# Seven products of half blocks for gate and up in a hybrid decoder layer

## The chip, the cores and the metric

One core of one Trainium2 chip runs the whole layer as one program. The metric is the device time of one execution in microseconds (us). Engines are named as in the profile: PE (matrix engine), PEld (its weight loads), DVE (vector), ACT (scalar), POOL, SP (which issues most DMAs).

## The reference, cut to what matters

512 tokens, width 1024, one layer, all arrays float32. The attention part in front is the same in both kernels; the change lies in what follows it (2816 hidden columns, that is 22 blocks of 128).

```python
mix = jnp.concatenate([o_a..., o_b...], axis=-1)
h = h + mix @ w_out[layer]
hn = rms_norm(h, norm2_g[layer])
h = h + (jax.nn.silu(hn @ w_gate[layer]) * (hn @ w_up[layer])) @ w_down[layer]
return rms_norm(h, norm_f_g)
```

## The kernel before

**Products in three matmuls.** Every float32 operand is split into a high part (rounded to the fp32r type, a copy on ACT) and a low part (the rest, a subtraction on DVE). A product is then three matmuls, high by high, high by low and low by high, which one PSUM bank adds up: `mm3` (lines 87 to 91, the weight is the stationary operand) and `mm3x` (93 to 97, the activation is). Each matmul has its own load of 128x128 stationary values. `split` (78 to 85) loads 128x512 raw weights by SP and splits them; the letters in `ENG` say which engine does which half.

**Out projection (587 to 604).** Eight steps f, each 128 rows of h1 (features on partitions, 512 tokens in the free dimension). A step loads a partial sum from DRAM (`hp`), does 4 x 3 matmuls of 512 columns, adds on DVE (596), and makes the scaled high and low parts `Xh`, `Xl` on ACT and DVE (598, 599). `turn` (580) transposes h1 on PE to `h1t` (tokens on partitions).

**Gate and up (643 to 666).** For each of 22 blocks j: gate, then up, each 8 x 3 matmuls of 512 columns (`gate_up`, 48 matmuls for a block), with four raw loads of 128x512. `swiglu` (652) does four steps on DVE, a Silu and a copy on ACT, and leaves high and low parts `GH[j]`, `GL[j]`. `second_norm` (626) squares `h1t` on ACT, takes the reciprocal root and spreads it to `R2`, by which both results are multiplied.

**Down (698 to 713).** Two halves c of the 1024 output columns, one after the other; in each, 22 steps k with 4 token tiles x 3 matmuls of 512 columns into four PSUM banks. The last four k are done token tile by token tile, so that `combine` and `finish` of a tile lie beside the next tile's matmuls.

The order of the instructions on each engine comes from a scheduler that the program is built with; tile pools with a fixed number of buffers (`BUFS`, line 39) say how far loads and splits run ahead.

Of the kernel before, what the change touches and what calls it, by code (L numbers as in the profile page):

```python
# [38 lines left out]
BUFS = {"w_raw": 3, "w_hl": 5, "pf": 2, "P": 2, "T": 2, "mf": 1, "oc": 1, "g": 4, "h1": 5, "pair": 1}  # L39
# [13 lines left out]
def tile_hybrid_layer(ctx: ExitStack, tc: tile.TileContext, xT, w_qk0, w_t, w_av, w_vb, w_o, w_gu, w_d,  # L53
# [33 lines left out]
    def mm3(ps, w, sl, xh, xl, first, last):  # L87

        nc.tensor.matmul(ps, w[:, 0, sl], xh, start=first, stop=False)  # L89
        nc.tensor.matmul(ps, w[:, 0, sl], xl, start=False, stop=False)  # L90
        nc.tensor.matmul(ps, w[:, 1, sl], xh, start=False, stop=last)  # L91
# [210 lines left out]
    mixh = act.tile([P, KT, S], F32R, name="act_hi")  # L302
    mixl = act.tile([P, KT, S], F32R, name="act_lo")
# [73 lines left out]
    def blocks(i, wi, tok):  # L377
# [12 lines left out]
        rhl = (mixh if wi == 0 else mixl)[:, 4:8].rearrange("p (x g) s -> p x g s", x=2)  # L390
# [91 lines left out]
    def out_a(f, tok):  # L482
# [3 lines left out]
        for ft in range(4):  # L486
            mm3(ps, w, slice(ft * P, (ft + 1) * P), mixh[:, ft], mixl[:, ft], ft == 0, ft == 3)
# [99 lines left out]
    for f in range(KT):  # L587
        xr = ff.tile([P, S], F32, name="g", bufs=BUFS["g"])
        nc.sync.dma_start(xr, hp[f * P:(f + 1) * P, :])
        w = split(w_o[f, :, 512:1024], 512, *ENG["ob"][:2])  # L590
        ps = bank(("proj", "S")[f % 2])
        for ft in range(4, KT):
            mm3(ps, w, slice((ft - 4) * P, (ft - 3) * P), mixh[:, ft], mixl[:, ft], ft == 4, ft == KT - 1)
        h1 = ff.tile([P, S], F32, name="h1", bufs=BUFS["h1"])
        h1s.append(h1)
        nc.vector.tensor_tensor(out=h1, in0=ps, in1=xr, op=ALU.add)
        g = g_sb[:, 1, f:f + 1]
        nc.scalar.activation(Xh[:, f], h1, AF.Copy, scale=g)
        nc.vector.scalar_tensor_tensor(out=Xl[:, f], in0=h1, scalar=g, in1=Xh[:, f].bitcast(F32), op0=ALU.mult,
                                       op1=ALU.subtract)  # L600
        if f >= DELAY:
            turn(f - DELAY)
    for f in range(KT - DELAY, KT):
        turn(f)
# [56 lines left out]
    for j in range(NJ):
        pg = gate_up(j, 0)
        if j == 0:
            second_norm()
        pu = gate_up(j, 1)
        swiglu(j, pg, pu)


    gf = ff.tile([P, D], F32, name="Xh", bufs=1)
    nc.sync.dma_start(gf, gf_row.to_broadcast([P, D]))  # L670
# [121 lines left out]
```

## Time and profile before

| | |
|---|---|
| three timed runs | 678.35, 681.23, 682.34 us, median 681.23 us |
| the profiled execution | 679.24 us, of which the span of the page is 677.5 us |
| PE busy | 657.1 us, 97% of the span, 3150 matmuls |
| DVE, ACT, POOL busy | 381.5, 305.5, 143.8 us |
| HBM traffic | 106 GB/s over the span |

Matmuls overlap each other in the records, so a busy PE is read by the distance from one start to the next, not by the duration of one. The same holds on DVE where nothing is waited for.

### The profile page before, as it was taken

What the parts mean: (1) busy time and instruction counts of PE and PEld (TensorE: products, weight loads), DVE (VectorE), ACT (ScalarE), POOL (GpSimd) and SP (SyncE); (2) the same over time, 40 slices, a digit from 0 to 9 for tenths busy, and PEclk for the clock granted to TensorE, in tenths of its full rate; (3) what the DMA queues carried; (4) which work ended last, traced back from release to release, by engine and by line L of the source; (5) the groups of instructions that cost most, each with busy time, mean ns of one, the idle gap of its engine ahead of it and who ended that gap; (6) DMA issues with size and microseconds to landing.
All of it is one profiled execution on the core that took longest, in us unless ns stands there. A gap on an engine that the chain in (4) does not pass through costs nothing.

```text
span 677.5 us, 9409 instructions
## 1 busy us (share of the span) xinstructions
PE 657.1 (97%) x3150; PEld 547.0 (81%) x3150; DVE 381.5 (56%) x828; ACT 305.5 (45%) x668; POOL 143.8 (21%) x184
## 2 busy tenths in 40 slices
PE   9999997999999999899999999999999999999995
PEld 6888897888878887778888888888888888888884
DVE  4468776777877679484645555445445532243225
ACT  5544565436765678466433333333333322232214
POOL 6635842253355455320000000000000000000000
PEclk9999998989999999999999999999999999999998
DMA  6766666445236640062222222222223232213213
GB/s 187 225 172 187 174 171 162 126 138 160 79 110 167 208 121 5 1 228 83 94 94 104 98 94 94 100 103 93 94 94 104 98 124 94 93 66 120 94 48 124
DMA packets 47180, 80.13 MB, mean 118 GB/s; under 512 B 7019, under 2 KB 10347, under 8 KB 47132
## 3 DMA queue, kind: packets, MB, share of 16 engines
q1 hardware_dynamic: 46556, 78.48, 37.2%
q10 hardware_dynamic: 576, 1.05, 0.4%
q8 instruction: 25, 0.41, 0.3%
q14 instruction: 23, 0.19, 0.1%
HBM read 66.36 MB, written 5.55 MB: 106 GB/s over the span
## 4 chain that ended last, share of the span: by engine, by line
PE 92%; DVE 3%; ACT 2%; DMA 1%; issue 1%; SPq 0%; ACTq 0%; DVEq 0%
PE proj L89 9%; PE proj L90 9%; PE proj L91 9%; PE PT L89 5%; PE PT L90 5%; PE PT L91 5%; PE S L89 4%; PE S L90 4%; PE S L91 4%; PE PT L340 3%; PE proj L96 2%; PE proj L95 2%; PE proj L97 2%; PE PT L96 2%; PE PT L95 2%; PE PT L97 2%
## 5 line engine op out<-in xcount | busy, mean ns | idle before, releaser
L71 ACT CAST w_hl<-w_raw 128x512 fp32r<-128x512 f32 (+2 forms) x187 | 112.2, 603 | 261.5 <-PE PT L91 62.9
L84 DVE TENSOR_TENSOR w_hl<-w_raw,w_hl 128x512 fp32r<-128x512 f32 (+1 forms) x169 | 116.9, 693 | 145.1 <-ACT w_hl L71 144.6
L84 POOL TENSOR_TENSOR w_hl<-w_raw,w_hl 128x512 fp32r<-128x512 f32 (+1 forms) x47 | 60.9, 1301 | 63.5 <-ACT w_hl L71 26.1
L337 POOL TENSOR_SCALAR P<-P,den 128x512 f32<-128x512 f32 (+1 forms) x96 | 51.5, 558 | 39.1 <-DVE den L329 27.4
L325 ACT ACTIVATE P<-P,mn 128x512 f32<-128x512 f32 (+1 forms) x96 | 53.5, 559 | 12.7 <-DVE mn L323 12.5
L89 PE MATMUL PT<-Xh,w_hl 128*128 128x512 f32 x144 | 56.0, 389 | 0.0
L90 PE MATMUL PT<-Xl,w_hl 128*128 128x512 f32 x144 | 56.0, 389 | 0.0
L91 PE MATMUL PT<-Xh,w_hl 128*128 128x512 f32 x144 | 56.0, 389 | 0.0
L76 DVE TENSOR_TENSOR PTl<-PT,PTh 128x512 fp32r<-128x512 f32 (+2 forms) x96 | 43.8, 482 | 9.7 <-ACT PTh L350 9.3
L323 DVE CUSTOM_DVE_ANT_0 P<-S,T 128x512 f32<-128x512 f32 (+1 forms) x96 | 44.0, 483 | 8.6 <-PE S L318 7.1
L350 ACT CAST PTh<-PT 128x512 fp32r<-128x512 f32 (+2 forms) x96 | 38.1, 426 | 22.3 <-PE PT L340 18.3
L89 PE MATMUL proj<-xh,w_hl 128*128 128x512 f32 x112 | 45.9, 410 | 0.0
L90 PE MATMUL proj<-xl,w_hl 128*128 128x512 f32 x112 | 45.2, 403 | 0.0
L91 PE MATMUL proj<-xh,w_hl 128*128 128x512 f32 x112 | 45.1, 403 | 0.0
L91 PE MATMUL S<-Xh,w_hl 128*128 128x512 f32 x104 | 40.9, 393 | 0.0
L89 PE MATMUL S<-Xh,w_hl 128*128 128x512 f32 x104 | 40.7, 392 | 0.0
L90 PE MATMUL S<-Xl,w_hl 128*128 128x512 f32 x104 | 40.5, 389 | 0.0
L89 PE MATMUL proj<-Xh,w_hl 128*128 128x512 f32 x104 | 40.5, 389 | 0.0
L90 PE MATMUL proj<-Xl,w_hl 128*128 128x512 f32 x104 | 40.5, 389 | 0.0
L91 PE MATMUL proj<-Xh,w_hl 128*128 128x512 f32 x104 | 40.5, 389 | 0.0
L340 PE MATMUL PT<-ident,P 128*128 128x128 f32 x240 | 36.0, 273 | 0.8 <-POOL P L337 0.8
L340 PEld LDWEIGHTS PT<-ident,P 128*128 128x128 f32 x240 | 28.3, 140 | 5.1 <-POOL P L337 1.3
(275 smaller groups left out, 1423.4 us busy)
## 6 DMA issues: line engine op xcount, KB each, us to landing
w_raw<-in_w_gu_dram SPq DMA_DIRECT2D x88, 256.0 KB, 2.7
w_raw<-in_w_d_dram SPq DMA_DIRECT2D x44, 256.0 KB, 2.8
w_raw<-in_w_t_dram SPq DMA_DIRECT2D x28, 256.0 KB, 2.9
T<-gd SPq DMA_DIRECT2D x64, 64.0 KB, 2.0
w_raw<-in_w_o_dram SPq DMA_DIRECT2D x16, 256.0 KB, 3.0
w_raw<-in_w_vb_dram SPq DMA_DIRECT2D x16, 140.0 KB, 2.2
Qb<-in_xT_dram SPq DMA_DIRECT2D x8, 256.0 KB, 3.0
w_raw<-in_w_av_dram SPq DMA_DIRECT2D x8, 256.0 KB, 2.8
```

What stands on the lines that cost most here:

```text
L71: nc.scalar.copy(out, in_)
L76: engines[e].tensor_tensor(out=out, in0=in0, in1=in1, op=op)
L84: engines[lo].tensor_tensor(out=w[:, 1, :n], in0=raw[:, :n], in1=w[:, 0, :n].bitcast(F32), op=ALU.subtract)
L89: nc.tensor.matmul(ps, w[:, 0, sl], xh, start=first, stop=False)
L90: nc.tensor.matmul(ps, w[:, 0, sl], xl, start=False, stop=False)
L91: nc.tensor.matmul(ps, w[:, 1, sl], xh, start=False, stop=last)
L95: nc.tensor.matmul(ps, xh, w[:, 0, sl], start=first, stop=False)
L323: nc.vector.tensor_tensor_reduce(out=pp, in0=sv, in1=T[:, S - w:], op0=ALU.add, op1=ALU.min, scale=1.0, scalar=3e38, accum_out=mn[:, t:t + 1])
L325: nc.scalar.activation(pp, pp, AF.Exp, bias=mn[:, t:t + 1], scale=-1.0, accum_out=den[:, t:t + 1])
L337: nc.gpsimd.tensor_scalar(pp, pp, den[:, t:t + 1], 1.0, op0=ALU.mult, op1=ALU.mult)
L340: nc.tensor.transpose(pv[:, kb * P:(kb + 1) * P], pp[:, kb * P:(kb + 1) * P], ident)
L350: nc.scalar.copy(ov[0], pv)
```

## The change

The attention part keeps its instructions (two tiles are cut in four, with other names). In the feed-forward part:

- **Seven products.** The gate and up weights of a block and the two halves of the 1024 features are taken as a 2x2 matrix of blocks, the features by the two halves of the tokens as another. Instead of eight block products (128 columns out, 512 features, 256 tokens) there are seven, of sums and differences of blocks. So a block j has 7 x 4 x 3 = 84 matmuls of 256 columns instead of 48 of 512.
- **Sums of weights.** `weights(j)` loads the same four 128x512 pieces, forms four sums of them on DVE, and splits seven pieces instead of four, four of them in pairs of 128x1024.
- **Blocks of x.** `lower` and `upper` make the seven blocks of x from h1 in the out projection, in place of `Xh` and `Xl`: per f<4 two scaled copies and one cast on ACT and four steps on DVE, per f>=4 one scaled copy and one cast of 768 columns on ACT and five steps on DVE, all beside the add of h1.
- **Results.** Partial sums stay in PSUM and are added to by later products; three of them are copied out by ACT, five steps of 256 columns and one of 512 on DVE finish a block. The result stays in fp32; `split_g` splits it in the down stage.
- **Down.** One pass over k with both column halves, so all eight PSUM banks are in use; w_down is loaded as 128x1024. h1t goes to DRAM after the second norm (four DMAs of 512 KB) and comes back in the down stage.

```diff
-BUFS = {"w_raw": 3, "w_hl": 5, "pf": 2, "P": 2, "T": 2, "mf": 1, "oc": 1, "g": 4, "h1": 5, "pair": 1}
+BUFS = {"w_raw": 3, "w_hl": 5, "pf": 2, "P": 2, "T": 2, "mf": 1, "oc": 1, "g": 3, "h1": 4, "pair": 1, "raw2": 6, "hl2": 3, "xe": 4, "xf": 4}
...
+    def lower(k):
+
+        h, g, n = h1s[k], g_sb[:, 1, k:k + 1], ng[:, k:k + 1]
+        e = ff.tile([P, 2, HS], F32, name="xe", bufs=BUFS["xe"])
+        nc.scalar.activation(e[:, 1], h[:, HS:], AF.Copy, scale=g)
+        nc.vector.scalar_tensor_tensor(out=e[:, 0], in0=h[:, :HS], scalar=n, in1=e[:, 1], op0=ALU.mult, op1=ALU.add)
+        nc.scalar.activation(X1[0][:, k, 0], h[:, :HS], AF.Copy, scale=n)
+        nc.vector.scalar_tensor_tensor(out=X1[1][:, k, 0], in0=h[:, :HS], scalar=n, in1=X1[0][:, k, 0].bitcast(F32),
+                                       op0=ALU.mult, op1=ALU.subtract)
+        copy("a", X1[0][:, k, 1], e[:, 0])
+        tt("v", X1[1][:, k, 1], e[:, 0], X1[0][:, k, 1].bitcast(F32), ALU.subtract)
+        return e
+
+    def upper(k, e):
...
+        nc.vector.scalar_tensor_tensor(out=f[:, 0], in0=h[:, HS:], scalar=g, in1=e[:, 0], op0=ALU.mult, op1=ALU.subtract)
+        nc.vector.scalar_tensor_tensor(out=f[:, 1], in0=h[:, HS:], scalar=n, in1=e[:, 1], op0=ALU.mult, op1=ALU.add)
+        nc.vector.scalar_tensor_tensor(out=f[:, 2], in0=h[:, :HS], scalar=g, in1=f[:, 0], op0=ALU.mult, op1=ALU.subtract)
+        b = X2[0][:, k, 0:2].rearrange("p a n -> p (a n)")
+        nc.scalar.activation(b, h, AF.Copy, scale=n)
+        nc.vector.scalar_tensor_tensor(out=X2[1][:, k, 0:2].rearrange("p a n -> p (a n)"), in0=h, scalar=n,
+                                       in1=b.bitcast(F32), op0=ALU.mult, op1=ALU.subtract)
+        copy("a", X2[0][:, k, 2:5], f)
+        tt("v", X2[1][:, k, 2:5], f, X2[0][:, k, 2:5].bitcast(F32), ALU.subtract)
...
+    def weights(j):
+
+        l0 = raw2()
+        nc.sync.dma_start(l0[:, 0], w_gu[j, 0, :, 0:WC])
...
+        tt("v", l0[:, 1], c, d, ALU.add)
+        w0 = split2(l0, "a", "v")
+        yield {"a": w0[:, :, 0], "S1": w0[:, :, 1]}
+        l1, l2 = raw2(), raw2()
+        nc.sync.dma_start(l1[:, 1], w_gu[j, 0, :, WC:])
+        tt("v", l1[:, 0], l0[:, 1], l0[:, 0], ALU.add)
+        w1 = split2(l1, "a", "v")
+        tt("v", l2[:, 0], l1[:, 0], l1[:, 1], ALU.add)
+        tt("v", l2[:, 1], c, l0[:, 0], ALU.add)
+        yield {"S2": w1[:, :, 0], "b": w1[:, :, 1], "S4": split1(l2[:, 0], "a", "v"), "S3": split1(l2[:, 1], "a", "v"),
+               "d": split1(d, "a", "v")}
+
+    def product(ps, w, X, b, first):
+
+        for k in range(HK):
+            mm3(ps, w, slice(k * P, (k + 1) * P), X[0][:, k, b], X[1][:, k, b], first and k == 0, k == HK - 1, True)
...
+        product(u["A"], u["w"]["a"], X1, 0, True)
+        nc.scalar.copy(u["q1"], u["A"])
+        product(u["C"], u["w"]["S1"], X1, 1, True)
+        nc.scalar.copy(u["p5"], u["C"])
+        return u
+
+    def second_part(j, u):
...
+        product(u["A"], u["w"]["S2"], X2, 2, False)
+        nc.scalar.copy(u["u2"], u["A"])
+        product(u["B"], u["w"]["b"], X2, 0, True)
+        tt("v", y[:, :HS], u["B"], u["q1"], ALU.add)
+        product(u["C"], u["w"]["S4"], X2, 1, False)
+        tt("v", y[:, HS:], u["C"], u["u2"], ALU.add)
+        product(u["A"], u["w"]["S3"], X2, 3, False)
+        tt("v", z[:, HS:], u["A"], u["p5"], ALU.add)
+        tt("v", y, y, R2, ALU.mult)
+        nc.scalar.activation(y, y, AF.Silu, scale=-1.0)
+
+    def third_part(j, u):
+        y, z = u["y"], zs[j]
+        product(u["A"], u["w"]["d"], X2, 4, False)
+        tt("v", z[:, :HS], u["A"], y[:, :HS], ALU.mult)
+        tt("v", z[:, HS:], z[:, HS:], y[:, HS:], ALU.mult)
...
+    second_part(0, units[0])
+    third_part(0, units[0])
+    for j in range(1, NJ):
+        if j > 1:
+            units[j] = first_part(j)
+            third_part(j - 1, units[j - 1])
+        second_part(j, units[j])
+    third_part(NJ - 1, units[NJ - 1])
...
+        copy("a", GH[k], zs[k])
+        tt("v", GL[k], zs[k], GH[k].bitcast(F32), ALU.subtract)
...
+        if k < NJ - LAST:
+            for c in range(2):
+                for t in range(NT):
+                    down(ps, t, c, k, w)
```

How the change moves instructions, at the three places that the prediction speaks of.

DVE at the end of the out projection, before: `h_...` is h1 of one f, `Xl` the low parts, `w_hl` low parts of weights, `h1t` the transposed h1.

```order
L596 TENSOR_TENSOR h_3511<-proj,g 128x512
L84 TENSOR_TENSOR w_hl<-w_raw,w_hl 128x512
L599 SCALAR_TENSOR_TENSOR Xl<-h_3511,g_sb,Xh 128x512
L596 TENSOR_TENSOR h_3541<-S,g 128x512
L73 COPY h1t<-PT 128x4x128
L84 TENSOR_TENSOR w_hl<-w_raw,w_hl 128x512
L599 SCALAR_TENSOR_TENSOR Xl<-h_3541,g_sb,Xh 128x512
```

The same place now (`X_3331` holds the low parts of five of the blocks, `xf` the sums they come from, `raw_3681` the weights of block j=1):

```order
L651 TENSOR_TENSOR h_3597<-S,g 128x512
L632 SCALAR_TENSOR_TENSOR xf<-h_3561,g_sb,xe 128x256
L633 SCALAR_TENSOR_TENSOR xf<-h_3561,ng,xe 128x256
L634 SCALAR_TENSOR_TENSOR xf<-h_3525,g_sb,xf 128x256
L637 SCALAR_TENSOR_TENSOR X_3331<-h_3561,ng,X_3330 128x512
L76 TENSOR_TENSOR X_3331<-xf,X_3330 128x768
L632 SCALAR_TENSOR_TENSOR xf<-h_3597,g_sb,xe 128x256
L633 SCALAR_TENSOR_TENSOR xf<-h_3597,ng,xe 128x256
L634 SCALAR_TENSOR_TENSOR xf<-h_3561,g_sb,xf 128x256
L637 SCALAR_TENSOR_TENSOR X_3331<-h_3597,ng,X_3330 128x512
L76 TENSOR_TENSOR X_3331<-xf,X_3330 128x768
L634 SCALAR_TENSOR_TENSOR xf<-h_3597,g_sb,xf 128x256
```

From the last add of h1 to the last low part of x there were three steps; now there are thirteen and a tiny one (two more of 768 columns follow the rows shown), and only then come the sums of the weights of block 1.

ACT at the same place now (`g,ss<-h1t` are the squares of the second norm, `h1t<-PT` the copies of the transposes, `X_3330` high parts of blocks, `xf<-S` a partial sum from PSUM):

```order
L636 ACTIVATE X_3330<-h_3597,ng 128x512
L71 COPY h1t<-PT 128x4x128
L71 CAST X_3330<-xf 128x768
L657 ACTIVATE g,ss<-h1t 128x512 x4
L721 COPY xf<-S 128x256
L723 COPY xf<-proj 128x256
L657 ACTIVATE g,ss<-h1t 128x512 x2
L71 CAST X_3330<-xf 128x768
L657 ACTIVATE g,ss<-h1t 128x512
L71 CAST X_3330<-xf 128x768
```

The casts of the last two steps' high parts (k=2 and 3) stand behind six and seven squares; before, the last high part of x stood ahead of all squares but one.

DVE in the middle of gate and up, before, one block j (`G_3573` is a result's low part):

```order
L84 TENSOR_TENSOR w_hl<-w_raw,w_hl 128x512
L76 TENSOR_TENSOR g<-S,R_3570 128x512
L84 TENSOR_TENSOR w_hl<-w_raw,w_hl 128x512
L76 TENSOR_TENSOR g<-g,R_3570 128x512
L84 TENSOR_TENSOR w_hl<-w_raw,w_hl 128x512
```

And now, most of one block (`raw_...` sums of weights, `hl_...` low parts of a pair, `act_...` the fp32 result):

```order
L76 TENSOR_TENSOR raw_5432<-w_raw,raw_5421 128x512
L76 TENSOR_TENSOR g<-proj,xf 128x256
L76 TENSOR_TENSOR g<-g,R_3337 128x512
L76 TENSOR_TENSOR hl_5301<-raw_5294,hl_5301 128x1024
L76 TENSOR_TENSOR raw_5421<-w_raw 128x512
L76 TENSOR_TENSOR raw_5431<-raw_5421 128x512
L76 TENSOR_TENSOR act_3772<-S,xf 128x256
L76 TENSOR_TENSOR raw_5432<-raw_5431 128x512
L76 TENSOR_TENSOR w_hl<-raw_5305,w_hl 128x512
L76 TENSOR_TENSOR act_3772<-act_3772,g 128x256
L76 TENSOR_TENSOR g<-PT,xf 128x256
L76 TENSOR_TENSOR hl_5308<-raw_5304,hl_5308 128x1024
```

A block had eight DVE steps of 512 columns; it has fifteen now: eight of 512, two of 1024, five of 256, and steps that wait for PE stand between those that make the next block's weights.

## Rows read from the trace of the kernel before

**Rows 1.** The page: busy time of the engines, and the chain that ended last by engine.
```profile
PE 657.1 (97%) x3150; PEld 547.0 (81%) x3150; DVE 381.5 (56%) x828; ACT 305.5 (45%) x668; POOL 143.8 (21%) x184
...
PE 92%; DVE 3%; ACT 2%; DMA 1%; issue 1%; SPq 0%; ACTq 0%; DVEq 0%
```
**Rows 2.** Windows: gate and up, then down; busy us and count by engine, granted clock, DMA.
```profile
304.78:544.60 239.82, 239.82 (x1063) 198.30 (x1062) 123.27 (x194) 90.95 (x156) 0.00 (x0) 1.00 0.28 96
544.60:669.30 124.70, 124.70 (x536) 100.11 (x534) 39.65 (x65) 33.34 (x61) 0.00 (x0) 1.00 0.26 89
```
**Rows 3.** PE in order of time, gate and up: start, us, instruction (22 matmuls, 21 steps).
```profile
360.22 0.39 PE L91 MATMUL PT<-Xh,w_hl 128*128 128x512 f32 x1
...
364.98 0.39 PE L91 MATMUL S<-Xh,w_hl 128*128 128x512 f32 x1
```
**Rows 4.** PE in order of time, narrower matmuls: 280 columns (nine steps), then 256.
```profile
126.02 0.29 PE L97 MATMUL proj<-w_hl,xl 128*128 128x280 f32 x1
...
127.17 0.29 PE L97 MATMUL proj<-w_hl,xl 128*128 128x280 f32 x1
...
128.06 0.28 PE L317 MATMUL S<-KDb,Qb 128*128 128x256 f32 x1
128.18 0.28 PE L318 MATMUL S<-KL,Qb 128*128 128x256 f32 x1
```
**Rows 5.** One line's instructions: weight loads of the 280-column matmuls, ns min/median/max.
```profile
L95 PEld LDWEIGHTS proj<-w_hl,xh x48: 186/188/193, 14.1 to 131.2; 128*128 128x128 f32 x48
```
**Rows 6.** Groups by form on DVE: busy us, mean ns, idle before and its releaser.
```profile
L84 DVE TENSOR_TENSOR w_hl<-w_raw,w_hl 128x512 fp32r<-128x512 f32 x70 | 48.5, 693 | 47.2 <-ACT w_hl L71 46.9
...
L76 DVE TENSOR_TENSOR PTl<-PT,PTh 128x256 fp32r<-128x256 f32 x24 | 10.0, 416 | 0.5 <-ACT PTh L350 0.5
...
L76 DVE TENSOR_TENSOR act_hi<-Qb,act_hi 128x1024 fp32r<-128x1024 f32 x1 | 1.2, 1225 | 0.1
```
**Rows 7.** DVE in order of time: steps that wait for nothing, in three places.
```profile
134.70 0.47 DVE L282 SCALAR_TENSOR_TENSOR vb<-proj,rstd_t,vb 128x256 fp32r<-128x256 f32 x1
135.09 0.41 DVE L323 CUSTOM_DVE_ANT_0 P<-S,T 128x256 f32<-128x256 f32 x1
...
178.99 0.42 DVE L76 TENSOR_TENSOR PTl<-PT,PTh 128x256 fp32r<-128x256 f32 x1
179.33 0.42 DVE L458 TENSOR_TENSOR cy<-S,cy 128x256 f32<-128x256 f32 x1
...
300.49 0.68 DVE L84 TENSOR_TENSOR w_hl<-w_raw,w_hl 128x512 fp32r<-128x512 f32 x1
301.09 0.74 DVE L599 SCALAR_TENSOR_TENSOR Xl<-h,g_sb,Xh 128x512 fp32r<-128x512 f32 x1
301.75 0.68 DVE L596 TENSOR_TENSOR h<-proj,g 128x512 f32<-128x512 f32 x1
```
**Rows 8.** Out projection: DVE's first add of h1, PE's last matmul there, its first of gate.
```profile
290.39 0.69 DVE L596 TENSOR_TENSOR h<-proj,g 128x512 f32<-128x512 f32 x1 [4.84 <-PE proj L91]
...
303.76 0.39 PE L91 MATMUL S<-act_hi,w_hl 128*128 128x512 f32 x1
...
304.78 0.47 PE L89 MATMUL S<-Xh,w_hl 128*128 128x512 f32 x1
```
**Rows 9.** ACT in order of time: two squares of the second norm.
```profile
311.31 0.62 ACT L612 ACTIVATE g<-h1t 128x512 f32<-128x512 f32 x1
...
311.92 0.61 ACT L612 ACTIVATE g<-h1t 128x512 f32<-128x512 f32 x1
```
**Rows 10.** Windows in front of the out projection's last steps.
```profile
284.00:286.20 2.20, 0.21 (x1) 0.00 (x0) 0.68 (x1) 1.20 (x2) 0.00 (x0) 0.99 0.00 0
286.20:289.60 3.40, 3.35 (x8) 2.69 (x9) 0.00 (x0) 0.39 (x1) 1.27 (x1) 0.50 0.29 64
```
**Rows 11.** The end, in order of time: PE's last matmul and the last DMA issue.
```profile
668.98 0.40 PE L97 MATMUL O<-w_hl,G 128*128 128x512 f32 x1
...
673.61 0.37 ACTq L688 DMA_DIRECT2D out_dram<-h1t  x1
```

More of the change, by code (lines that the diff above doesn't have):

```diff
@@ L85, in split, with mm3 @@
         return w
[L87 to L91, printed above, removed]
+    def mm3(ps, w, sl, xh, xl, first, last, skip=False):
+        nc.tensor.matmul(ps, w[:, 0, sl], xh, start=first, stop=False, skip_group_check=skip)
+        nc.tensor.matmul(ps, w[:, 0, sl], xl, start=False, stop=False, skip_group_check=skip)
+        nc.tensor.matmul(ps, w[:, 1, sl], xh, start=False, stop=last, skip_group_check=skip)
     def mm3x(ps, xh, xl, w, sl, first, last):
@@ L594, in tile_hybrid_layer @@
         h1 = ff.tile([P, S], F32, name="h1", bufs=BUFS["h1"])
-        h1s.append(h1)
+        h1s[f] = h1
         nc.vector.tensor_tensor(out=h1, in0=ps, in1=xr, op=ALU.add)
[L597 to L604, printed above, removed]
@@ L661, in tile_hybrid_layer @@
[L661 to L670, printed above, removed]
-    def w_down(k, c):
-        return split(w_d[k * P:(k + 1) * P, c * HD:(c + 1) * HD], HD, *ENG["d"])
-    def down(ps, t, k, w):
-        tk = slice(t * P, (t + 1) * P)
-        mm3x(ps[t], GH[k][:, tk], GL[k][:, tk], w, slice(0, HD), k == 0, k == NJ - 1)
@@ new lines, in second_part @@
+    def second_part(j, u):
+        if j == 16:
+            Z = ff.tile([P, KT, S], F32, name="h1t", bufs=1)
+            zs.extend(Z[:, i] for i in range(NJ - 16))
+        y, z = u["y"], zs[j]
[9 more added lines that the diff above has]
+        nc.scalar.activation(y, y, AF.Silu, scale=-1.0)
@@ new lines, in third_part @@
+    def third_part(j, u):
+        y, z = u["y"], zs[j]
+        product(u["A"], u["w"]["d"], X2, 4, False)
+        tt("v", z[:, :HS], u["A"], y[:, :HS], ALU.mult)
+        tt("v", z[:, HS:], z[:, HS:], y[:, HS:], ALU.mult)
+    es = []
+    for f in range(KT):
+        out_b(f)
+        if f < HK:
+            es.append(lower(f))
+        else:
+            upper(f - HK, es[f - HK])
+            done = nc.cur_bb.bb.instructions[-1]
+        if f >= DELAY:
+            turn(f - DELAY)
+        if f == 2:
+            ahead = weights(0)
+            w0 = next(ahead)
@@ new lines, in tile_hybrid_layer @@
+    for f in range(KT - DELAY, KT):
+        turn(f)
+    w0.update(next(ahead))
+    units = {0: first_part(0, w0)}
+    with tc.issue_after(done):
+        units[1] = first_part(1)
+    second_norm()
+    quads = ["act00", "act01", "act10", "act11"]
+    zs = [q[:, i] for tag in quads for q in [act.tile([P, 4, S], F32, name=tag)] for i in range(4)]
+    second_part(0, units[0])
[5 more added lines that the diff above has]
+        second_part(j, units[j])
@@ new lines, in tile_hybrid_layer @@
+    for t in range(NT):
+        for c in range(2):
+            for i, k in enumerate(range(NJ - LAST, NJ)):
+                down(ps, t, c, k, ws_last[i])
+            x = cell(t, c)
+            nc.vector.scalar_tensor_tensor(out=x, in0=ps[c][t], scalar=nrstd_t[:, t:t + 1], in1=x, op0=ALU.mult,
+                                           op1=ALU.add)
+            square(t, c, x)
+            if c == 0:
+                tt(ENG["c"], x, x, gf[0], ALU.mult)
+        rsqrt(slice(t, t + 1), rstd_t)
```

174 lines of the change are left out of this document (101 added, 73 removed), and 2 rows, old and new, of the table ENG.

## The prediction

> **What bounds the kernel now.** I read the page first: PE is busy for 97% of the span, and the chain that ended last is PE for 92% [rows 1]. So the time is PE's stream of matmuls plus a few gaps, and the other engines matter where they make PE wait. The windows by stage show that nothing does so in the two stages that are changed: gate and up is one unbroken run of 239.82 us, down one of 124.70 us, at the full clock, with DVE busy for 123.27 us and ACT for 90.95 us of the first [rows 2]. A busy PE says nothing about its pace, so I took that from start to start: 21 steps in 4.76 us, 0.2267 us for a matmul of 512 columns [rows 3]. The attention part keeps its instructions and their order, so I leave it alone.
>
> **PE's work in gate and up.** Before: 22 blocks x 48 = 1056 matmuls x 0.2267 = 239.4 us, which is the window [rows 2]. Now: 22 x 84 = 1848 matmuls of 256 columns. The stage has none of that width, but attention does: two stand 0.12 us apart, and nine steps of 280 columns take 1.15 us, 0.1278 each [rows 4]. Taking off 24 columns at the pace that lies between 280 and 512 (0.0989 us for 232 columns, 0.43 ns each) gives 0.1176. I take 0.118: 218.1 us, a gain of 21.3 us. Bounds: 0.117 (216.2 us, gain 23.2) and 0.1278, since narrower can't be slower than 280 columns (236.2 us, gain 3.2).
>
> What speaks against this: the weight loads grow from 1056 to 1848. A load of the 280-column matmuls lasts 0.188 us [rows 5], yet those matmuls follow each other after 0.1278 us, so loads overlap each other as well as matmuls, and a load's duration is not its price. The Trainium skill (Perfetto Trace Analysis, Identifying the Most-Contended Engine) says that the busy share of weight loads, not of matmuls, is the measure of how near PE is to its limit. By that rule 1848 loads of 0.188 us, 347 us, would be the stage, and the change a large loss; the rows above speak against it, and it is a rival below.
>
> **DVE's work in gate and up.** A block has fifteen steps: eight of 512 columns, two of 1024, five of 256. By their durations, 0.693, 1.225 and 0.416 us [rows 6], that is 10.07 us, against 84 x 0.118 = 9.91 us of PE: DVE would be the bound. But the duration is the distance only where a step waits. Where steps wait for nothing, the next starts 0.60 us after one of 512 columns, 0.34 after one of 256 [rows 7], some 0.08 us sooner; for 1024 I take 1.14. That makes 4.80 + 2.28 + 1.70 = 8.8 us, about 9.1 with two steps a block that need the one before them. So DVE is 92% busy where it was half busy. The Trainium skill (VectorE: DVE Perf Modes, The DRAIN you can't avoid) says that a step does not start until the pipe of the one before is empty. By it a block would cost the 10.07 us; the rows show the earlier starts, so I keep 9.1, and 10.07 is the upper bound.
>
> The weight buffers hold about one block ahead, so small waits are absorbed. Price of what is not: between 0 and (10.07 - 9.91) x 21 = 3.4 us, more if waits come on top (a rival). I take 2.
>
> **The start of gate and up.** Here I see the largest loss. Before, DVE followed PE closely through the out projection, and gate began 1 us after the last matmul there [rows 8]. Now DVE has, from its first add of h1 at 290.39 [rows 8], 49 steps before the last block of x is split: 15 plain ones of 512 columns, 20 scaled ones of 256, 4 scaled ones of 512, 4 plain ones of 256, 2 of 1024, 4 of 768. At spacings of 0.60, 0.39, 0.66, 0.34 [rows 7], 1.14 and about 0.87 (between 512 and 1024) this is 9.0 + 7.8 + 2.6 + 1.4 + 2.3 + 3.5 = 26.6 us: 317 us on this trace's clock if it never waits. It does wait: the last two casts on ACT stand behind the squares, at 0.62 us each [rows 9], so I put the last low part at 320.
>
> PE is through with the out projection at 304. Until 320 it can do only what block 0 offers, 72 matmuls (8.5 us) and four groups of transposes (1.6 us; two such groups fill the 0.8 us between the stages [rows 8]), the last 15 of them after 320, so it reaches 322 with some 8 us lost. Behind that DVE makes the weights of blocks 1 and 2 (another 20 steps or so, until about 333), which PE could use sooner: some 3.5 us more. I take 11.5 us lost. Bounds: 4 us, if ACT and DVE overlap better than I counted and PE fills in, and 20 us, if waits on ACT stretch the 49 steps by a third. PE idles in pieces; when it idled for 2.2 us before, the granted clock was 0.50 for the next 3.4 us and eight matmuls took them all [rows 10], which is inside the upper bound.
>
> **The rest.** Down keeps its 528 matmuls: 124.70 us for the window, 0.2327 us each with edges [rows 2]. A step k now has 24 of them, 5.6 us, against 1.225 + 0.693 = 1.9 us on DVE [rows 6] for splits of 1024 and 512 columns, and two copies of the same widths on ACT, so the splits are hidden, and three steps' weights are split before the 18 late results come. If that cover went, it would show as PE gaps at k=3. The pace went from 0.227 in gate to 0.233 in down with the same shapes, so other buffers may move it by 0.006 either way, 3 us; I take 0. Joining the stages costs nothing now; the last product of block 21 waits for DVE once, beside which down's first matmuls are queued: 0.5 us. From PE's last matmul to the last issue were 4.6 us [rows 11], by the same kinds of steps: 0. The four stores of h1t and their reloads stand in SP's queue ahead of loads for block 2 and k=12; both are needed some 8 us later: 0, or 1 us in the ramp, inside its bounds.
>
> **Sum.** -21.3 + 2 + 11.5 + 0.5 = -7.3 us on the profiled execution's own 679.24 us: 672 us. That execution lies 2 us under the median of the runs shown, 681.23, and within their range.
>
> **Rivals.**
> - *PE is hardly held at the start*: 4 us instead of 11.5, no loss in the blocks. For it: DVE idled 4.84 us before its first add of h1 [rows 8], so the stage had room. -21.3 + 4 + 0.5 gives 662 us, with the lower bound of the matmuls 660.
> - *DVE sets the pace, mildly*: a block takes 10.2 us, the durations of rows 6 and a little waiting. 21 x 0.29 = 6 us instead of 2: 676 to 678 us, no change that can be told.
> - *DVE sets the pace with waits* (the other side): PE's results and the next weights stand in one DVE queue. A step that waits for PE holds up the weights behind it, PE then comes late, and the next step waits again. It decides from a block time of 10.25 us (7.3 us over 21 blocks, beside the 2 that I gave); with one such wait of 0.5 us on top of 10.07 it is 10.57, 14 us over 21 blocks instead of 2: 684 us. For it: DVE's mean wait behind an ACT cast is already 0.67 us a step before (47.2 us, 70 steps [rows 6]). Against it: the buffers hold a block.
> - *Weight loads set the pace*, as the rule on their busy share has it: 1848 x 0.188 = 347 us, 107 us more than before, some 786 us. Only the 280-column rows stand against it, and they are enough for me.
>
> **How the numbers follow.** 0.5% is about what a measurement of this kernel can tell from no change, 3.4 us. The forecast (667 to 676) has 0.46, little loss at the start 0.21, mild DVE pace 0.15, DVE pace with waits 0.16, weight loads 0.02. Faster: 0.46 + 0.21 and a little of the mild case, 0.68; same 0.14; slower 0.18. The forecast's own range is 667 to 676; to hold 8 in 10 it reaches down to most of the first rival, 661, and up through the mild case to the third rival's price, 684.
>
> **What would show it.** Right: about 1848 matmuls of 256 columns, 0.118 us apart; DVE over 85% busy in gate and up; PE gaps that end on DVE low parts between 304 and 335 us of the span, few later; a block of 9.9 to 10 us. Wrong: a block of over 10.25 us with PE waiting for DVE throughout, matmuls more than 0.125 us apart without a gap, or a down stage that is not 123 to 126 us.

## The result, and the profile after

The changed kernel takes 671.51 us (median of 4 runs, 670.78 to 672.42) beside 680.45 us (678.35 to 682.34) of the kernel before: a ratio of 0.987, 95% interval 0.9836 to 0.9903. A second set of runs, taken later, gave 0.9869 (0.9846 to 0.9893). It is faster by 1.3%, 9 us; the prediction was 672.0.

The page of the changed kernel (span 669.5 us), busy times and the chain that ended last, to be read against [rows 1]:

```profile
PE 640.4 (96%) x3942; PEld 570.6 (85%) x3942; DVE 478.1 (71%) x994; ACT 353.1 (53%) x745; POOL 143.5 (21%) x184
...
PE 84%; DVE 7%; ACT 3%; issue 2%; DMA 1%; POOL 0%; SPq 0%; DVEq 0%; ACTq 0%; POOLq 0%
```

PE still has most of the chain, but 84% of it where it had 92%; DVE and ACT have taken over that part. Where they did so is seen in windows: the start of gate and up in two pieces, the steady middle, and down (columns as in [rows 2]).

```profile
304.60:322.00 17.40, 12.81 (x76) 11.96 (x74) 15.36 (x28) 14.57 (x33) 0.00 (x0) 0.71 0.31 122
322.00:345.00 23.00, 21.86 (x175) 20.77 (x174) 23.00 (x43) 15.04 (x25) 0.00 (x0) 1.00 0.37 126
```
```profile
400.00:500.00 100.00, 100.00 (x846) 100.00 (x845) 92.68 (x152) 53.99 (x91) 0.00 (x0) 1.00 0.32 109
```
```profile
545.00:661.90 116.90, 114.46 (x498) 93.06 (x497) 46.35 (x64) 37.98 (x58) 0.00 (x0) 1.00 0.25 88
```

In the middle PE does 846 matmuls in 100 us, 0.118 us each, without a gap, and DVE is 93% busy beside it. In the first 17.4 us PE does 76 matmuls where that pace would give 147, at a mean clock of 0.71. The list of what PE waited for (us in total, times, longest) over the whole feed-forward part is short:

```profile
PE PT L612 <- DVE h L651: 3.3, 1, 3.3
PE S L96 <- DVE hl L76: 1.6, 1, 1.6
PE PT L90 <- DVE X L637: 1.3, 1, 1.3
PE S L95 <- ACT hl L71: 0.8, 1, 0.8
PE proj L91 <- DVE hl L76: 0.6, 1, 0.6
PE S L89 <- ACT xf L721: 0.5, 1, 0.5
PE S L89 <- ACT xf L732: 0.5, 1, 0.5
```

The first, the third and the last lie at the start; the second and fourth (L95 and L96 are the down stage) at step k=3 of down; the other two are single waits in later blocks, at 342 and 365 us. The start in more detail, windows first, then DVE's last steps for x in order of time:

```profile
309.00:312.45 3.45, 0.12 (x3) 0.03 (x1) 3.45 (x7) 1.43 (x3) 0.00 (x0) 0.81 0.00 0
312.45:316.90 4.45, 3.22 (x14) 2.92 (x14) 4.45 (x10) 3.94 (x10) 0.00 (x0) 0.50 0.45 178
316.90:321.40 4.50, 4.48 (x19) 4.24 (x20) 2.46 (x5) 4.48 (x13) 0.00 (x0) 0.50 0.74 294
```
```profile
311.62 0.68 DVE L651 TENSOR_TENSOR h<-S,g 128x512 f32<-128x512 f32 x1
...
319.86 0.96 DVE L76 TENSOR_TENSOR X<-xf,X 128x768 fp32r<-128x768 f32 x1 [1.73 <-ACT X L71]
...
321.21 0.96 DVE L76 TENSOR_TENSOR X<-xf,X 128x768 fp32r<-128x768 f32 x1 [0.32 <-ACT X L71]
322.08 0.68 DVE L76 TENSOR_TENSOR raw<-w_raw 128x512 f32<-128x512 f32 x1
```

PE waits from 309 to 312.45: the transposes of the last step's h1 are next in its queue, and the last add of h1 comes only at 311.62, 7.0 us after PE began the last matmul of the out projection (304.58): it stands in DVE's queue behind steps for x and for the weights of block 0. Then the granted clock is 0.50 for some 10 us, and DVE finishes the last x block at 322.2.

A balance, worked out from the starts of the matmuls in the two traces. From the first matmul of gate to the last of down it was 364.20 us and is 356.77, 7.4 us less; the rest of the 8.0 us between the spans lies in front (the first matmul comes 0.4 us later) and behind (from the last matmul to the end 7.6 us, before 8.5). Groups of 84 matmuls, one block's worth, from start to start:

```
21.05 10.76 10.67 9.96 10.70 9.99 9.97 9.97 9.97 9.97 9.96 ... 9.97 9.96 us
```

| | before | after | difference, us |
|---|---|---|---|
| gate and up at their steady pace | 1056 x 0.2267 = 239.4 | 1848 x 0.1186 = 219.2 | -20.2 |
| gate and up beyond that pace (nearly all in the first six groups) | 1.9 | 13.8 | +11.9 |
| down at its pace, from its first start to its last | 122.9 (0.233 a matmul) | 121.0 (0.230) | -1.9 |
| down, waits at k=3 | 0 | 2.8 | +2.8 |
| sum | 364.2 | 356.8 | -7.4 |

### The profile page after: what moved, and what is told of

The parts are those of the page before. It is cut to its first block, busy times and chain, and to the rows that moved or that the text cites. A ratio compares the mean times of both kernels' runs of the same rounds, so it can differ in the third digit from the quotient of the medians.

```text
span 669.5 us, 11165 instructions
## 1 busy us (share of the span) xinstructions
PE 640.4 (96%) x3942; PEld 570.6 (85%) x3942; DVE 478.1 (71%) x994; ACT 353.1 (53%) x745; POOL 143.5 (21%) x184
## 4 chain that ended last, share of the span: by engine, by line
PE 84%; DVE 7%; ACT 3%; issue 2%; DMA 1%; POOL 0%; SPq 0%; DVEq 0%; ACTq 0%; POOLq 0%
PE proj L89 8%; PE proj L91 8%; PE proj L90 8%; PE S L89 6%; PE S L90 6%; PE S L91 6%; PE PT L340 3%; PE proj L96 3%; PE proj L95 3%; PE proj L97 3%; PE PT L96 2%; PE PT L97 2%; PE PT L95 2%; PE PT L89 2%; PE PT L90 2%
## 5 line engine op out<-in xcount | busy, mean ns | idle before, releaser
L76 DVE TENSOR_TENSOR hl<-raw,hl 128x1024 fp32r<-128x1024 f32 x64 | 77.8, 1219 | 53.7 <-ACT hl L71 49.2
L71 ACT CAST hl<-raw 128x1024 fp32r<-128x1024 f32 x64 | 67.1, 1051 | 61.9 <-PE O L97 57.5
L71 ACT CAST w_hl<-w_raw 128x512 fp32r<-128x512 f32 (+2 forms) x76 | 43.3, 576 | 59.9 <-PE S L91 18.9
L325 ACT ACTIVATE P<-P,mn 128x512 f32<-128x512 f32 (+1 forms) x96 | 53.5, 559 | 12.6 <-DVE mn L323 12.3
L76 DVE TENSOR_TENSOR PTl<-PT,PTh 128x512 fp32r<-128x512 f32 (+2 forms) x96 | 43.8, 482 | 9.6 <-ACT PTh L350 9.2
L89 PE MATMUL S<-X,hl 128*128 128x256 f32 x176 | 50.0, 284 | 0.5 <-ACT xf L721 0.5
L89 PE MATMUL S<-X,w_hl 128*128 128x256 f32 x176 | 49.7, 283 | 0.5 <-ACT xf L732 0.5
L90 PE MATMUL S<-X,w_hl 128*128 128x256 f32 x176 | 49.8, 283 | 0.0
L90 PE MATMUL S<-X,hl 128*128 128x256 f32 x176 | 49.7, 282 | 0.0
L91 PE MATMUL S<-X,w_hl 128*128 128x256 f32 x176 | 49.7, 283 | 0.0
L91 PE MATMUL S<-X,hl 128*128 128x256 f32 x176 | 49.5, 281 | 0.0
L71 ACT CAST w_hl<-raw 128x512 fp32r<-128x512 f32 x45 | 27.3, 619 | 35.5 <-PE S L91 28.3
L90 PE MATMUL proj<-xl,w_hl 128*128 128x512 f32 x112 | 45.5, 406 | 0.0
L84 DVE TENSOR_TENSOR w_hl<-w_raw,w_hl 128x512 fp32r<-128x512 f32 (+1 forms) x37 | 26.0, 708 | 14.7 <-ACT w_hl L71 14.4
L89 PEld LDWEIGHTS S<-X,hl 128*128 128x128 f32 x176 | 33.9, 192 | 0.9 <-ACT xf L721 0.9
```

Of the source, the lines that this page charges most:

```text
L71: nc.scalar.copy(out, in_)
L76: engines[e].tensor_tensor(out=out, in0=in0, in1=in1, op=op)
L84: engines[lo].tensor_tensor(out=w[:, 1, :n], in0=raw[:, :n], in1=w[:, 0, :n].bitcast(F32), op=ALU.subtract)
L325: nc.scalar.activation(pp, pp, AF.Exp, bias=mn[:, t:t + 1], scale=-1.0, accum_out=den[:, t:t + 1])
```

## The experiments

Two theories of the loss at the start stood against each other: DVE's steps for x hold PE (the prediction), or something beside them does, namely the fall of the clock, ACT's squares, or late transfers. Two more questions were the price of a narrow matmul and how near DVE is to setting the pace. Where a difference is under 2 us, the distance from the first matmul of gate to the last of down is given beside the ratio (356.8 us for the changed kernel, 357.3 in its second profile), since the first matmul of gate lies anywhere from 302.9 to 307.9 us from one profile to another (308.2 in experiment 9, whose edit reaches in front of it).

**1. The price of halves alone.** The kernel before, its 512-column matmuls cut in two:

```diff
-                mm3(ps, w, slice(k * P, (k + 1) * P), Xh[:, kt], Xl[:, kt], kt == 0, kt == KT - 1)
+                for b in (slice(0, S // 2), slice(S // 2, S)):
+                    mm3(ps[:, b], w, slice(k * P, (k + 1) * P), Xh[:, kt, b], Xl[:, kt, b], kt == 0, kt == KT - 1)
...
```

> The kernel before, with every 512-column matmul of gate and up made as two of 256 columns, so 2112 matmuls and 2112 weight loads in place of 1056; nothing is left out. PE pace theory: a matmul of 256 columns costs 0.118 to 0.119 us, so the stage takes 249 to 251 us in place of 239.4, and the kernel 10 to 11 us longer than the one before: 690 to 692 us beside 680.5. Weight-load theory (a load of 0.188 us is the price): 2112 x 0.188 = 397 us, some 157 us longer, about 838 us.

Measured: 1.0186 of the kernel before (1.0159 to 1.0212), 11 to 14 us longer, a little more than expected. One thing the expectation leaves unsaid: both halves sum in one bank with a start of their own, and gate and up come out with other values; the number, size and loads of the matmuls are as stated. Gate and up in one window:

```profile
304.00:560.00 256.00, 256.00 (x2124) 255.06 (x2123) 126.25 (x197) 92.73 (x160) 0.00 (x0) 1.00 0.29 92
```

The weight loads are busy for 99.6% of it and yet the matmuls follow each other after 0.120 us, though a load lasts 0.19 us. So 1056 more loads with the same columns cost 14 us (378.1 us from first to last matmul, 364.2 before), not 157: the rival in which the duration of the loads sets the pace is out. It also shows the price of the change's shape: a half costs 0.1186 to 0.120 us, not half of 0.2267, so seven eighths of the work bring 8.4% and not 12.5%.

**2. Without the low parts of x.** Of `lower` and `upper` the four steps that make low parts go, and the product reads the high part twice:

```diff
-        nc.vector.scalar_tensor_tensor(out=X1[1][:, k, 0], in0=h[:, :HS], scalar=n, in1=X1[0][:, k, 0].bitcast(F32),
-                                       op0=ALU.mult, op1=ALU.subtract)
...
-        tt("v", X2[1][:, k, 2:5], f, X2[0][:, k, 2:5].bitcast(F32), ALU.subtract)
...
-            mm3(ps, w, slice(k * P, (k + 1) * P), X[0][:, k, b], X[1][:, k, b], first and k == 0, k == HK - 1, True)
+            mm3(ps, w, slice(k * P, (k + 1) * P), X[0][:, k, b], X[0][:, k, b], first and k == 0, k == HK - 1, True)
```

> The changed kernel without the low parts of the seven x blocks: the sixteen DVE steps that make them are left out, and the matmuls that read them read the high parts instead, so PE's work is the same and the result is less exact. DVE theory (its steps ahead of the last x block hold PE): 8 x 0.37 + 4 x 0.66 + 4 x 0.87 = 9.1 us less on DVE before PE can go on, so the loss of some 12 us at the start falls to about 3 to 4: 661 to 664 us. Rivals in which DVE is not what holds PE (late raw weights, ACT's order, the clock): 669 to 672 us.

Measured: 0.9822 (0.9783 to 0.986), 670.45 us; 354.1 us from first to last matmul. About 3 us, not 9: the expectation missed, and the windows show why.

```profile
304.60:322.00 17.40, 16.56 (x135) 15.88 (x134) 14.23 (x25) 17.37 (x38) 0.00 (x0) 1.00 0.61 214
322.00:345.00 23.00, 17.23 (x119) 15.74 (x118) 18.79 (x37) 11.39 (x18) 0.00 (x0) 0.85 0.25 91
```

PE does 135 matmuls until 322 in place of 76, as the theory has it (some of them because gate begins 2.3 us sooner in this profile), but then 119 in place of 175. In order of time on PE:

```profile
327.11 0.39 PE L89 MATMUL S<-X,w_hl 128*128 128x256 f32 x1 [1.39 <-DVE act L76]
...
333.19 2.08 PE L137 MATMUL O<-g,ones 128*128 128x512 f32 x2 [4.38 <-DVE g L134]
```

L137 spreads the second norm's factors. It stands in PE's queue ahead of work that could run, and its input is made by the last (L134) of six DVE steps, five of them tiny, which stand between large ones from 321 to 333. Taking one wait away uncovered the next. Nor did all of the gain fall at the start: PE's waits at k=3 of down are gone in this run too, and down is 1.4 us shorter (2.8 us of waits less, at a slower pace, as in experiment 10), so the start itself gave back only 1.3 of the 2.7 us.

**3. PE kept busy.** 32 matmuls that nobody reads, where PE waits:

```diff
+    full = filler(14, last_pe())
+    with tc.issue_after(full):
+        turn(KT - 1)
+    full = filler(18, last_pe())
...
```

> The changed kernel with 32 added matmuls of 512 columns whose result nobody reads, 14 ahead of the transposes of the last h1 step and 18 behind them (7.3 us of PE), put where PE waits at the start of gate and up; nothing is left out. Clock theory: the 10.2 us at half clock there are the loss, matmuls took 0.213 us in place of 0.118; with the clock kept up the kernel gains 3 to 4.5 us: 667 to 668.5 us. DVE theory: PE can go on only when DVE has split the last x block at about 322 of the span, whatever its clock until then: 671 to 672.5 us, with the granted clock at 1.00 from 309 to 322.

Measured: 0.9871 (0.985 to 0.9893), as the changed kernel; 357.2 us from first to last matmul, also the same.

```profile
308.00:312.45 4.45, 4.45 (x36) 4.22 (x35) 4.45 (x9) 3.47 (x7) 0.00 (x0) 1.00 0.01 4
312.45:316.90 4.45, 4.03 (x21) 3.09 (x20) 4.45 (x10) 2.67 (x4) 0.00 (x0) 1.00 0.00 0
316.90:322.00 5.10, 5.10 (x33) 4.57 (x32) 3.99 (x7) 5.07 (x16) 0.00 (x0) 1.00 0.72 287
```

The clock stays at 1.00, 7.3 us of useless matmuls are taken in, and the time does not change. That the fill itself is not the new limit is seen in one wait that is left: PE still waits 0.6 us for the last low part of x (L90 for DVE's L76). So the half clock of the changed kernel cost nothing that this can tell: PE ran slowly in time that it had to wait in anyway. The changed kernel's second profile agrees: its clock over 304.6 to 322 is 0.80 in place of 0.71, and from first to last matmul it takes 357.3 us in place of 356.8.

**4. Squares behind the casts.**

```diff
...
-    second_norm()
+    with tc.issue_after(cast):
+        second_norm()
```

> The changed kernel with the squares of the second norm queued on ACT behind the last cast of an x block; nothing is left out. ACT theory: the casts behind the squares are the larger part of the loss, 5 us or more back: under 667 us. DVE theory: only the 1.73 and 0.32 us for which DVE waited for these casts come back, 1 to 2 us: 669.5 to 670.5 us; and R2 comes later, so a new wait of PE for results of blocks 0 and 1 may take it back: then 671.5 us or above.

Measured: 0.9874 (0.9856 to 0.9893), no gain; 358.6 us from first to last matmul, 1.8 more. PE's waits:

```profile
PE PT L612 <- DVE h L651: 3.3, 1, 3.3
PE S L89 <- ACT xf L732: 1.8, 1, 1.8
...
PE S L91 <- DVE hl L76: 1.4, 1, 1.4
PE O L137 <- DVE g L134: 1.0, 1, 1.0
...
PE PT L90 <- DVE X L637: 0.3, 1, 0.3
```

The wait for x falls from 1.3 to 0.3 us, and in its place stand a wait for the norm (L137) and two others. ACT's order by itself is not the loss.

**5. Both taken away: low parts and second norm.** Kernel 2 without `square`, `rsqrt` and `spread` in `second_norm`, factors set to ones.

> The changed kernel without the low parts of the x blocks and without the second norm (squares, reciprocal root, the matmul that spreads R2 and its copy are left out, R2 and the token factors are ones); the matmuls of the products stay. Theory: at the start DVE's steps ahead of the last x block and, behind them, the second norm's chain of small DVE steps hold PE one after the other; with both gone PE loses 1 to 4 us of the 12 between the out projection and 345 of the span, 8 to 11 us less than the changed kernel: 0.971 to 0.975 of the kernel before. Rival, raw weights that arrive late behind the stores of h1t, or ACT's casts, hold it as well: PE still waits 5 us or more there, 0.977 or above.

Measured: 0.9706 (0.9683 to 0.973), 661.07 us; 344.2 us from first to last matmul, 12.6 less than the changed kernel. The only waits of PE left in the feed-forward part, and the two windows:

```profile
PE PT L89 <- ACT hl L71: 0.2, 1, 0.2
PE S L89 <- ACT hl L71: 0.2, 1, 0.2
```
```profile
304.60:322.00 17.40, 17.01 (x134) 16.16 (x133) 16.89 (x31) 14.46 (x26) 0.00 (x0) 1.00 0.41 154
322.00:345.00 23.00, 23.00 (x196) 23.00 (x195) 21.76 (x38) 13.92 (x23) 0.00 (x0) 1.00 0.48 152
```

134 and 196 matmuls, though gate begins 2.3 us later in this profile: nothing is left of the loss, so late transfers are no third cause, and ACT's casts of the x blocks, with no squares ahead of them here, hold nothing either. Of the 12.6 us, 1.4 lie in down, where the waits at k=3 are gone as in experiment 2; 11.2 lie at the start.

**6. Only the second norm taken away.**

> The changed kernel without the second norm alone (squares, reciprocal root, the matmul that spreads R2 and its copy are left out, R2 and the token factors are ones); the low parts of the x blocks stay. Together the two were worth 0.0163 of the kernel before, 11 us (0.9869 to 0.9706), the low parts alone 0.0047, 3 us. Theory, two limits one behind the other (first DVE's steps ahead of the last x block, then the norm's chain): without the norm alone the first limit stays, and only the 2.05 us that DVE waits for casts behind squares and 0.9 us of the spreading matmuls can come back, 1 to 4 us: 0.981 to 0.986. Rival, the two add up: the norm alone is worth 0.0163 - 0.0047, 8 us: 0.973 to 0.977.

Measured: 0.9825 (0.9801 to 0.9849); 353.6 us from first to last matmul. Low parts alone are worth 0.0047, the norm alone 0.0044, both together 0.0163 of 681 us, that is 3.2, 3.0 and 11.1 us. They do not add up: one stands behind the other, and removing either leaves most of the loss to its neighbour. The intervals of these ratios are wide beside the first two figures; the starts of the matmuls say it more sharply. At the start alone, with the 1.4 us of down taken off, low parts give 1.3 us, the norm 3.2, both together 11.2. Which part of the norm holds PE (squares, the small DVE steps or the spreading matmuls) this run does not separate; in experiment 2 the wait for it ends on DVE's step L134.

**7. and 8. One and two more DVE steps in each block.**

```diff
+        for _ in range(1 if j else 0):
+            tt("v", l2[:, 1], c, l0[:, 1], ALU.add)
         tt("v", l2[:, 1], c, l0[:, 0], ALU.add)
```

> The changed kernel with one more DVE step of 512 columns for each block from j=1 on (a sum of weights made twice); nothing is left out. PE theory for the steady part (a block takes PE 9.965 us, DVE is busy for 9.25 of them): 9.25 + 0.60 = 9.85 still fits, so blocks stay at 9.96 to 9.98 us and only the start, where DVE has work waiting, loses 1 to 3 us: ratio to the kernel before 0.988 to 0.992. Rival, DVE paces already (its waits are part of its pace): 0.6 us a block, 12 us in all: ratio 1.005.

> The changed kernel with two more DVE steps of 512 columns for each block from j=1 on; nothing is left out. DVE then needs 9.25 + 1.20 = 10.45 us a block and sets the pace: blocks of 10.45 to 10.6 us, 10 to 13 us more over 21 blocks, and 1 to 3 us at the start: ratio to the kernel before 1.004 to 1.010. If DVE had more slack than its busy share shows (steps overlap), blocks stay under 10.1 us: ratio under 0.993.

Measured: 0.990 (0.9873 to 0.9927) with one, 1.018 (1.0161 to 1.0199) with two. The same window of the steady middle, first with one, then with two:

```profile
400.00:500.00 100.00, 100.00 (x845) 100.00 (x844) 94.06 (x162) 53.09 (x90) 0.00 (x0) 1.00 0.33 106
```
```profile
400.00:500.00 100.00, 94.58 (x783) 92.57 (x781) 95.36 (x160) 51.35 (x84) 0.00 (x0) 1.00 0.33 103
```

With one, PE still does 845 matmuls, and blocks stay at 9.97 us. With two, blocks take 10.75 us, and PE waits in every block:

```profile
PE S L91 <- DVE hl L76: 11.8, 19, 0.9
PE S L95 <- ACT hl L71: 5.7, 1, 5.7
```

So the changed kernel has room for one step a block and not for two: DVE is hidden, just. The dose was larger than expected: 10.75 us, not 10.45 to 10.6, and the wait at k=3 of down (L95) grew from 0.8 to 5.7 us. DVE is busy for 95.4 of the 100 us, 10.25 of each 10.75. Most of the rest is no wait for PE, as the third rival would have it (0.9 us), but for raw weights. DVE's row for the steps that wait for them, same window (busy us, mean ns, idle before and its releaser):

```profile
L76 DVE TENSOR_TENSOR raw<-w_raw 128x512 f32<-128x512 f32 x10 | 6.9, 692 | 4.0 <-DMA w_raw<-in_w_gu_dram 3.8
```

Before SP issues such a load (line 697) it waits for a DVE step, 14.2 us in nine times over this window; so a DVE that runs late also gets its next weights late. The added steps read these buffers too.

**9. POOL helps at the start.** The four sums of weights of blocks 0 to 2:

```diff
-        tt("v", l0[:, 1], c, d, ALU.add)
+        e = "p" if j < 3 else "v"
+        tt(e, l0[:, 1], c, d, ALU.add)
...
```

> The changed kernel with the four sums of weights of blocks 0, 1 and 2 made by POOL, which is idle there, in place of DVE; nothing is left out. Twelve steps of 0.60 us leave DVE, four of them ahead of the last x block. DVE theory: PE goes on 2.4 us sooner and the weights of blocks 1 and 2 are less late: 2 to 5 us gained, ratio 0.980 to 0.984. Second theory (DVE is one of two limits at the start; behind it stand the six small steps of the second norm, the matmul that spreads R2, and raw loads behind the stores of h1t, as in the run without low parts of x): 0 to 2 us gained, ratio 0.984 to 0.987. Rival, POOL slows DVE when both work: DVE steps of 512 columns longer than 0.75 us, no gain.

Measured: 0.9945 (0.9926 to 0.9964), 5 us slower than the changed kernel. POOL's steps there, then DVE's at the same time:

```profile
297.72 4.35 POOL L76 TENSOR_TENSOR raw<-raw 128x512 f32<-128x512 f32 x3
...
319.81 3.42 POOL L76 TENSOR_TENSOR raw<-raw 128x512 f32<-128x512 f32 x2
```
```profile
297.97 1.50 DVE L620 SCALAR_TENSOR_TENSOR xe<-h,ng,xe 128x256 f32<-128x256 f32 x1
299.40 0.68 DVE L651 TENSOR_TENSOR h<-S,g 128x512 f32<-128x512 f32 x1
...
320.58 1.50 DVE L632 SCALAR_TENSOR_TENSOR xf<-h,g_sb,xe 128x256 f32<-128x256 f32 x1
322.00 1.50 DVE L633 SCALAR_TENSOR_TENSOR xf<-h,ng,xe 128x256 f32<-128x256 f32 x1
...
324.09 0.47 DVE L632 SCALAR_TENSOR_TENSOR xf<-h,g_sb,xe 128x256 f32<-128x256 f32 x1
```

While POOL works, a DVE step of 256 columns takes 1.50 us, about as long as one POOL step, in place of 0.47; when POOL stops at 323.2, it is 0.47 again. The add of h1 at 299.40, one of whose inputs comes from PSUM, is not held: 0.68 us, as ever. The Trainium skill (GPSIMD Engine Reference, Specifications) says that POOL's SBUF interfaces are shared with VectorE and contend with its steps that have two SBUF inputs; the rows agree on both counts. POOL's help costs DVE more than it saves, and the start, where DVE is the limit, is the worst place for it. Some of the loss lies in the out projection: from DVE's first add of h1 to the first matmul of gate it takes 16.8 us in place of 13.9.

**10. The weights ahead of the splits in down.** In the changed kernel the splits of the results wait until the x blocks are free, at 545, and then run in one piece on ACT, ahead of the weights that PE needs next (`hl`):

```profile
545.10 6.36 ACT L71 CAST X<-act 128x512 fp32r<-128x512 f32 x12 [7.59 <-PE S L90]
551.36 3.22 ACT L71 CAST X<-h1t 128x512 fp32r<-128x512 f32 x6
554.48 2.95 ACT L71 CAST hl<-raw 128x1024 fp32r<-128x1024 f32 x3
```

The edit queues the split of step k behind the weights of k-1:

```diff
-        split_g(k)
+        held = ExitStack()
+        if k > 3:
+            for i in ahead:
+                held.enter_context(tc.issue_after(i))
+        ahead = nc.cur_bb.bb.instructions[-2:]
+        with held:
+            split_g(k)
```

> The changed kernel with the splits of the results k=4 and later queued in the down stage behind the weight split of step k-1, on ACT and on DVE, in place of all in one piece ahead of the weights of k=3; nothing is left out. Theory: PE's two waits at 554 to 559 of the span (1.0 and 1.8 us, for weights of k=3 cast behind 18 casts) go: 2.5 to 3 us gained, ratio 0.982 to 0.984. Rival, the wait only moves (a result split late, or raw loads late): ratio 0.986 to 0.988.

Measured: 0.9854 (0.9834 to 0.9875), between the two; 355.1 us from first to last matmul, 1.7 less. Both waits of down are gone, but its pace is another: 0.2333 us in place of 0.229. Two matmuls of down, 21 steps apart, in order of time on PE, first of the changed kernel, then of this one:

```profile
599.92 0.39 PE L97 MATMUL PT<-hl,act 128*128 128x512 f32 x1
...
604.73 0.39 PE L97 MATMUL PT<-hl,act 128*128 128x512 f32 x1
```
```profile
600.01 0.40 PE L97 MATMUL PT<-hl,act 128*128 128x512 f32 x1
...
604.91 0.40 PE L97 MATMUL PT<-hl,act 128*128 128x512 f32 x1
```

4.81 us and 4.90 us for the same 21 steps. Over the stage this gives back 1.4 of the 2.8 us.

**11. A better version: an early first part of block 1, and experiment 10.**

```diff
-    with tc.issue_after(done):
-        units[1] = first_part(1)
+    next_up = weights(1)
+    w1 = next(next_up)
+    units[1] = first_part(1, w1)
+    with tc.issue_after(done):
+        w1.update(next(next_up))
```

> The changed kernel with two edits, nothing left out: the first two products of block 1, which need only x blocks of f below 4, are no longer queued on DVE behind the last x block (their weights cost DVE 0.60 + 1.14 us and give PE 24 matmuls, 2.8 us, to do where it waits), and the splits of the down stage are queued as in the run named e8_join. DVE theory: 1 us at the start; down 1.4 us as that run's trace showed (2.8 us of waits gone, 1.5 us given back by a pace of 0.233 us in place of 0.229): 2 to 3 us less than the changed kernel, 0.982 to 0.984 of the kernel before. Rival: the two added DVE steps push the last x block back by as much as PE gains: only the 1.4 us of down, 0.984 to 0.986.

The unaltered changed kernel ran beside it:

> The changed kernel, unaltered, beside the two others of this call on the same chip: 0.985 to 0.989 of the kernel before, as its own runs and the runs with little altered gave.

Measured: 0.9839 (0.9818 to 0.9859), 670.18 us, beside 0.9869 (0.9846 to 0.9893), 671.59 us. From first to last matmul 353.7 us, 3.0 to 3.5 less than the two profiles of the changed kernel, about half of it at the start. It is the fastest complete version here, and faster than the kernel before; against the changed kernel the intervals overlap, so 1.4 to 2 us is what the runs suggest, not what they prove.

## Why the prediction was right

- **PE's work in gate and up** (-21.3 us): right in kind, 1.1 us too good. 0.1186 us a matmul in place of 0.118 [rows 4]; experiment 1 shows nearly the same price, 0.120, without any of the change's other parts.
- **DVE in gate and up** (92% busy, hidden, 2 us): right. DVE is 92.7% busy in the middle, 9.24 us a block beside the 9.1 that was forecast; blocks take 9.97 us, inside the 9.9 to 10 that the prediction named, and experiments 7 and 8 put the limit between one and two more steps. Of the 2 us some 1.4 fell, not as small waits all along but as two single ones in the groups of 10.67 and 10.70 us: 0.6 us for a low part of weights from DVE, 0.5 us for ACT's copy of a partial sum. The group of 10.76 holds the two matmuls that spread the norm's factors (0.9 us), which the kernel before has too. In the table all this is part of the start. The rule that the prediction set against the early starts of DVE's steps (the Trainium skill, VectorE: DVE Perf Modes, The DRAIN you can't avoid) has its exception in the same paragraph, a next step that is not held starts earlier; the rows agree, with steps of 0.68 us 0.60 us apart [rows 7], so the 10.07 us was not what that paragraph gives for such steps.
- **The start of gate and up** (+11.5 us): right in size, 11.9 us in the table with the later waits in it, against 11.5 + 2. The window to 322 is 71 matmuls short of the steady pace, 8.4 us, where the prediction had some 8. The last low part of x was put at 320, and the trace has it at 321.2 to 322.2; the 49 steps are there, and so are the waits of 1.73 and 0.32 us for the casts behind the squares. Three points of the picture were off. The longest wait did not end on a low part but on the add of h1 for the last transposes, queued behind other DVE work; no run takes that wait away by itself. The 3.5 us behind 322 were put down to DVE's weights of blocks 1 and 2, and only one wait of 0.6 us ends on such weights. And the mechanism had one limit where there are two: experiments 2, 5 and 6 show the second norm's chain right behind the x blocks, for which the prediction has no term, so that 9 us less of DVE work alone brought 3 us, 1.3 of them at the start.
- **The clock** (inside the upper bound): it did fall, to 0.50 for 10 us, and experiment 3 shows no cost of it.
- **Down** (0, at most 3 either way) **and the joint** (0.5): the step that failed is "the splits are hidden". They were hidden by amount and not by order: 18 casts stood ahead of one set of weights, and PE waited 2.8 us at k=3, where the prediction had said such a gap would show. The stage's faster pace gave 1.9 back, so the sum came out at 0.9.
- **The sum**: -20.2 + 11.9 + 0.9, and -0.5 at the two ends, is -7.9 us, beside the -7.3 that was forecast. That the two lie so close is in part luck: the gain of PE's work was 1.1 us too good, the loss at the start and in the blocks 1.6 us too dear, and down and the two ends, 0.4 and 0.5 us off, cancel as well.
- **The rivals**: PE hardly held (662 us) is what experiment 5 gives, 661 us, with the work at the start taken out. A DVE pace with waits needs between 0.6 and 1.2 us more of DVE a block (experiments 7 and 8). Waits for PE in DVE's queue, by which that rival grew, were not what experiment 8 showed once DVE set the pace. The duration of weight loads as the limit is out (experiment 1): there the loads are busy for 99.6% of a stage that still runs at 0.120 us a matmul. The rule of the Trainium skill behind that rival (Perfetto Trace Analysis, Identifying the Most-Contended Engine) is not borne out as a price.

## What to carry to other kernels

Fewer products pay in the steady state only what the narrower matmul leaves, here 20 of 30 us, and what feeds the first of them has to be counted as a queue on one engine: the 49 DVE steps ahead of the last x block gave most of the size of the loss before any run. When a removed cost brings a third of its price, look for the next wait behind it and remove both: only the pair showed what the start was worth. A low clock or a long wait in a trace is no loss by itself; filling the time with idle work, and seeing that the end of the wait stays where it was, tells whether it was.

## What was not expected of the hardware

- POOL and DVE: a DVE step with two inputs from SBUF took 1.50 us in place of 0.47 beside a POOL step, and one of 512 columns with an input from PSUM 0.68 us as ever (experiment 9).
- Down has two paces. After a wait at k=3, in the changed kernel (both profiles) and experiments 3, 4, 6, 7, 8 and 9, the middle of the stage ran at 0.229 us a matmul; without one, in the kernel before and experiments 1, 2, 5, 10 and 11, at 0.2333. Kind and width of the instructions are the same; what sets the pace was not found.
- 2112 loads of 0.19 us, busy for 99.6% of a stage of 255 us, did not hold matmuls 0.120 us apart.
